# A hybrid diffusion backbone on one core: modulation sums on VectorE alone, five raw weight buffers, squares on ScalarE, and another order at the start of each block's second product

## The chip, the core and the metric

The kernel runs on one core of one Trainium2 chip. Its engines are TensorE (PE in the rows; its weight loads are PEld), VectorE (DVE), ScalarE (ACT), GpSimd (POOL), and SyncE (SP), which here only issues DMAs. The engines run side by side, each takes its own instructions strictly in the order of the program, and they wait for one another through semaphores. The metric is the time of the device in microseconds (us), the median over executions.

## What is computed

Two layers of a model over 512 latent tokens and 256 context tokens, of width 1024. Cut to what matters here:

```python
for layer in range(2):
    mod_x = silu(c) @ ada_w[layer] + ada_b[layer]        # 1024 x 6144 weights, for the latent tokens
    mod_c = silu(c_ctx) @ ada_w[layer] + ada_b[layer]    # the same weights, for the context tokens
    hx = rmsnorm(x, g1) * (1 + sc1) + sh1                # sh1, sc1, ... are sixths of mod_x
    x = x + gate1 * (mixer(hx) @ w_out[layer])           # retention and gated linear attention heads
    hx = rmsnorm(x, g2) * (1 + sc2) + sh2
    x = x + gate2 * (square(relu(hx @ w_mlp1[layer])) @ w_mlp2[layer])   # 1024 -> 4096 -> 1024
    # in layer 0 the context tokens go the same way, with mod_c
return rmsnorm(x)
```

All is float32. Products are made exact enough by splitting each operand into a rounded part (hi) and a remainder (lo), and adding three products: hi*hi, hi*lo, lo*hi. So each weight tile that lands raw has to be split: ScalarE makes hi by a cast, VectorE makes lo by a subtraction.

## The kernel before

Weights come in slabs of 128 x 1024 floats (512 KB). A slab is loaded by a DMA on SP's queue into one of NRAW = 4 raw buffers (pool `wraw`), and split into one of NSPL = 5 pairs of hi and lo buffers. `run` goes through a plan, a list of items in a fixed order; ahead of each item it splits slabs that later items need (`advance`), as far as a split buffer's last user has been issued, and loads slabs further ahead (`load_next`), as far as `limit = NRAW - (2 if ada_queue else 1) - order[loaded].raws` lets it: a slab counts as held from its load until its split is issued. The program order of every engine is the order in which this Python code issues.

The MLP of layer 0 is the stretch in question. Its 4096 hidden features are made in 8 blocks (u = 0 to 7) of 4 tiles of 128 features (m = 0 to 3). The first product of block u >= 1 is done by two pairs (`strassen_items`, a Strassen-Winograd scheme with seven products of half size): a pair takes two slabs of `w_mlp1` (`Pair`, two raw buffers at once, split in four parts) and makes two feature tiles for all 768 tokens. Its seven items in program order are p1, p6, p7, p5, p2, p4, p3. p1's bank of PSUM is copied to SBUF by ScalarE (line 1454) and p2 then adds to that bank; VectorE adds u2, u3, c22, c21 and c12 (line 1448), and p4 adds to the bank that u3 is read from. Each finished quarter goes through `hidden_chain`: relu on ScalarE (1425), the square rounded to hi on ScalarE (1426), the exact square on GpSimd (1427), lo = exact - hi on VectorE (1429). The second product of block u (`m2_part`) multiplies the 4 hidden tiles (its k tiles) by 4 slabs of `w_mlp2`; each slab holds two output tiles j. VectorE adds each result, times a gate, to the residual x (`residual`, line 641). Before, an item of the second product is one output tile in two banks (512 latent and 256 context tokens): in each bank first k = 0, 1, 2, then in each k = 3. Tiles k = 2 and 3 are those of the second pair, whose last quarter (c12) ends its chain last. In the last block an item is one output tile and one group of tokens.

Spread between these items is the modulation of layer 1 (`ada_sums`, called through `mlp_ada`): 64 tiles of `ada_w` (128 x 768, 384 KB, eight groups u of eight kk) are each loaded into a raw buffer and multiplied by a scalar per partition for each of the two conditions (v = 0, 1), and summed over kk; then nine small matmuls add over partitions. Before, v = 0 is summed by VectorE (405 for kk = 0, 407 after). For v = 1, ScalarE scales the tile (409 into a sum for kk < 2, else 411 in place, after VectorE has read it), and for kk >= 2 a DMA from GpSimd's queue adds the tile to one of two partial sums in SBUF (412). The load of the next tile is issued behind that. There are three calls of `mlp_ada` in each pair (after p6, p5 and p4) and eight in each second product of blocks 1 to 6. A group takes 11 calls: eight with a tile, two empty ones, and one with the small matmuls.

The other pools: `mp`, NSLOT = 47 slots of 768 floats per partition for activations, and PSUM with seven banks for products. `load_late` loads two constant tables, `delta` and `ramp`, once; `start` of each layer loads `cosT` and `sinT`.

Of the kernel before, what the change touches and what calls it, by code (L numbers as in the profile page):

```python
# [31 lines left out]
NSLOT = 47  # L32
NSPL = 5
NRAW = 4
# [103 lines left out]
def build(ctx: ExitStack, tc, a):  # L138
# [250 lines left out]
    def ada_sums(l):  # L389
        acc = [work(f"adaacc_{l}_{i}") for i in range(3)]  # L390
        todo = [(u, kk) for u in range(6 * D // T) for kk in range(KK)]

        def load(i):
            u, kk = todo[i]
            w = wraw.tile([P, WCOL], F32, tag="raw", name=f"adaw_{l}_{u}_{kk}")
            nc.sync.dma_start(w[:, 0:T], a["ada_w"][l, kk * P : (kk + 1) * P, u * T : (u + 1) * T])
            return w[:, 0:T]

        nxt = load(0)
        for i, (u, kk) in enumerate(todo):  # L400
            w = nxt
            c0, c1 = [cs[:, kk, v : v + 1] for v in range(2)]
            part = acc[1 + kk % 2]
            if kk == 0:
                nc.vector.tensor_scalar(acc[0], w, c0, None, op0=ALU.mult)
            else:
                nc.vector.scalar_tensor_tensor(acc[0], w, c0, acc[0], op0=ALU.mult, op1=ALU.add)  # L407
            if kk < 2:
                nc.scalar.mul(part, w, c1)
            else:  # L410
                nc.scalar.mul(w, w, c1)  # L411
                nc.gpsimd.dma_start(part, w, accum_op=ALU.add)  # L412
            if i + 1 < len(todo):
                nxt = load(i + 1)
            yield
            if kk == KK - 1:
                yield
                yield
                pt = psa.tile([P, 512], F32, tag="psa", name=f"ada_{l}_{u}")
                for j, v in enumerate((0, 1, 1)):  # L420
                    for c in range(3):
                        nc.tensor.matmul(
                            pt[32 * c : 32 * c + 32, 0:256], onehot[:, v], acc[j][:, 256 * c : 256 * c + 256],
                            start=(j == 0), stop=(j == 2),
                        )
                ada_state["end", l] = ch.start(ada_finish(l, pt, [6 * u + 2 * c for c in range(3)], 256))
                yield
# [278 lines left out]
    def load_late():  # L706
        for name, shape in (("delta", [P, P]), ("ramp", [P, 2, P])):
            late[name] = load_const(name, shape)
# [42 lines left out]
    def layer(l, norm):  # L751
# [11 lines left out]
        def start():  # L763
# [8 lines left out]
            tabs["ret"] = [pairs[h // 2][:, h % 2] for h in range(NH)]  # L772
            for name in ("cosT", "sinT"):
                late[name] = work(f"{name}_{l}")[:, 0:LAT]
                nc.sync.dma_start(late[name], a[name])
# [572 lines left out]
        def m2_part(u, jps, groups, last, batch=4):  # L1348


            def fn():
# [6 lines left out]
                for i in range(0, len(todo), batch):  # L1358
                    pts = [bank(f"pm2_{l}_{u}_{j}_{t0}") for j, s, c0, v, t0, t1 in todo[i : i + batch]]
                    for ks in (range(0, UT - 1), range(UT - 1, UT)):  # L1360
# [58 lines left out]
        def hidden_chain(c, a_, t0, relu):  # L1419
# [7 lines left out]
            nc.gpsimd.tensor_mul(c, c, c)  # L1427
# [74 lines left out]
        def m2_item(u, jps, groups=vwhole, last=False, ada=True, batch=4):  # L1502
# [3 lines left out]
                Item(f"m2.{u}.{jps}", m2_part(u, jps, groups, last, batch), [m2[u][x[0]] for x in jps])  # L1506
# [4 lines left out]
        if l == 0:  # L1511
# [20 lines left out]
            for u in range(1, NU):  # L1532
                for j in range(UT // 2 * u, UT // 2 * (u + 1)):
                    strassen_items(j)
                for q in tiles if u < NU - 1 else ():
                    m2_item(u, [q], batch=2)
            for g in range(2):
                for i, q in enumerate(tiles):
                    m2_item(NU - 1, [q], TG[g : g + 1], True)
                    if g == 1 and i == 1:  # L1540
# [167 lines left out]
```

## Time and profile before

| | before |
|---|---|
| median of 2 runs | 1837.45 us (1836.16 to 1838.75) |
| the profiled execution's own time | 1836.57 us |
| its span, first to last instruction | 1834.8 us |
| TensorE busy | 1653.0 us (90%), 9120 matmuls |
| VectorE busy | 1023.0 us (56%) |
| ScalarE busy | 735.2 us (40%) |
| GpSimd busy | 243.6 us (13%) |
| mean granted TensorE clock | 0.949 of 2.4 GHz |
| moved by DMA | 194.26 MB, mean 106 GB/s |

Times within the profile are counted from the start of the span. "Busy" is the time in which an engine has an instruction in work; matmuls overlap, so that a busy TensorE may still be below its peak. The idle time before an instruction is put down to the instruction or the DMA that ended it.

### The profile page before, as it was taken

The page shows a single profiled execution, that of the slowest core. Times are in us where ns is not written, and L with a number is a line of the kernel's source. Part 1 is how long each engine was busy: PE and PEld are TensorE (multiplying, and loading weights), DVE is VectorE, ACT ScalarE, POOL GpSimd, SP SyncE. Part 2 cuts the span into 40 slices and gives each one's busy share as a digit, 9 for nine tenths or more (in the row PEclk, how much of TensorE's full clock was granted, in tenths as well). Part 3 has the DMA queues.
Part 4 walks back from the last instruction along what each step waited for, and adds up shares of the span by engine and source line. Part 5 has one row for each costly group of instructions (what it writes and reads, how often), then busy time and mean ns, then how long its engine had stood idle before and what let it go on. Part 6 is the DMA issues. An engine that isn't in the chain of part 4 may idle for free. (4 is left out here: it accounts for less than half of the span.)

```text
span 1834.8 us, 23190 instructions
## 1 busy us (share of the span) xinstructions
PE 1653.0 (90%) x9120; PEld 1422.1 (78%) x9120; DVE 1023.0 (56%) x1656; ACT 735.2 (40%) x1231; POOL 243.6 (13%) x263
## 2 busy tenths in 40 slices
PE   6899999999997778797876788899999989999998
PEld 3678888888786767696866677778888988888887
DVE  6665754556864444565554554676856664334435
ACT  5526235635533332343423333646346442232322
POOL 2200111100201111111201111100121120010000
PEclk8999999999998979898888889999999999999999
DMA  9333431322135344365444352211213333322321
GB/s 333 105 128 137 136 106 63 108 72 71 56 91 128 97 113 121 109 179 132 128 114 104 101 150 103 92 52 58 69 47 104 104 108 99 103 92 92 104 81 46
DMA packets 67404, 194.26 MB, mean 106 GB/s; under 512 B 7296, under 2 KB 18880, under 8 KB 67296
## 3 DMA queue, kind: packets, MB, share of 16 engines
q1 hardware_dynamic: 58112, 166.42, 27.7%
q0 software_dynamic: 9184, 26.38, 7.0%
q8 instruction: 71, 1.16, 0.3%
q14 instruction: 37, 0.30, 0.0%
HBM read 169.70 MB, written 4.19 MB: 95 GB/s over the span
## 5 line engine op out<-in xcount | busy, mean ns | idle before, releaser
L532 PE MATMUL pm<-hidh,hi_m 128*128 128x512 f32 (+1 forms) x800 | 287.5, 359 | 40.0 <-ACT hidh L1426 40.0
L533 PE MATMUL pm<-hidl,hi_m 128*128 128x512 f32 (+1 forms) x800 | 286.6, 358 | 24.7 <-DVE hidl L1429 20.9
L534 PE MATMUL pm<-hidh,lo_m 128*128 128x512 f32 (+1 forms) x800 | 284.1, 355 | 0.0
L532 PEld LDWEIGHTS pm<-hidh,hi_m 128*128 128x128 f32 x800 | 157.1, 196 | 65.4 <-ACT hidh L1426 43.0
L533 PEld LDWEIGHTS pm<-hidl,hi_m 128*128 128x128 f32 x800 | 157.2, 196 | 48.0 <-DVE hidl L1429 24.0
L641 DVE SCALAR_TENSOR_TENSOR x<-pm,mod,x 128x512 f32<-128x512 f32 (+1 forms) x200 | 120.6, 641 | 131.0 <-PE pm L534 130.9
L534 PEld LDWEIGHTS pm<-hidh,lo_m 128*128 128x128 f32 x800 | 156.8, 196 | 19.9
L246 ACT CAST hi_m<-raw_m 128x1024 fp32r<-128x1024 f32 x100 | 104.0, 1040 | 106.5 <-PE pm L533 93.3
L411 ACT ACTIVATE adaw<-adaw,cs 128x768 f32<-128x768 f32 x48 | 44.9, 936 | 222.2 <-DVE adaacc L407 213.0
L247 DVE TENSOR_TENSOR lo_m<-raw_m,hi_m 128x1024 fp32r<-128x1024 f32 x98 | 120.1, 1226 | 23.1 <-ACT hi_m L246 19.9
L533 PE MATMUL pm<-yl,hi_m 128*128 128x512 f32 (+1 forms) x352 | 127.5, 362 | 2.1 <-DVE yl L627 2.1
L532 PE MATMUL pm<-yh,hi_m 128*128 128x512 f32 (+1 forms) x352 | 127.9, 363 | 0.0
L534 PE MATMUL pm<-yh,lo_m 128*128 128x512 f32 (+1 forms) x352 | 127.3, 362 | 0.5 <-DVE lo_m L247 0.5
L1327 DVE TENSOR_TENSOR hidl<-relu,hidh 128x512 fp32r<-128x512 f32 (+1 forms) x44 | 28.8, 658 | 159.8 <-POOL relu L1325 159.8
L1413 PE MATMUL pst<-yh,hi_m1s 128*128 128x384 f32 x224 | 82.2, 367 | 29.2 <-ACT p L1454 29.2
L407 DVE SCALAR_TENSOR_TENSOR adaacc<-adaw,cs,adaacc 128x768 f32<-128x768 f32 x56 | 58.1, 1038 | 76.4 <-DMA adaw<-in_ada_w 76.3
L412 POOL DMA_DIRECT2D adaacc<-adaw x48 | 42.3, 881 | 357.4 <-ACT adaw L411 253.7
L1325 POOL TENSOR_TENSOR relu<-relu 128x512 f32<-128x512 f32 (+1 forms) x44 | 42.3, 964 | 337.7 <-ACT hidh L1324 337.4
L1413 PE MATMUL pst<-yh,lo_m1s 128*128 128x384 f32 x224 | 80.5, 359 | 3.4 <-DVE lo_m1s L529 3.4
L1413 PE MATMUL pst<-yl,hi_m1s 128*128 128x384 f32 x224 | 80.2, 358 | 0.0
L247 DVE TENSOR_TENSOR lo_wi<-raw_wi,hi_wi 128x1024 fp32r<-128x1024 f32 x49 | 59.4, 1225 | 33.1 <-ACT hi_wi L246 33.1
L533 PEld LDWEIGHTS pm<-yl,hi_m 128*128 128x128 f32 x352 | 67.0, 190 | 12.9 <-DVE yl L627 2.9
(361 smaller groups left out, 4062.0 us busy)
## 6 DMA issues: line engine op xcount, KB each, us to landing
raw_m<-in_w_mlp SPq DMA_DIRECT2D x100, 512.0 KB, 3.5
raw_wi<-in_w_in SPq DMA_DIRECT2D x58, 512.0 KB, 3.5
adaw<-in_ada_w SPq DMA_DIRECT2D x64, 384.0 KB, 3.3
adaacc<-adaw POOLq DMA_DIRECT2D x48, 384.0 KB, 4.0
adaw<-in_ada_w SPq DMA_DIRECT2D x32, 512.0 KB, 4.6
raw_m1s<-in_w_mlp SPq DMA_DIRECT2D x28, 512.0 KB, 3.6
adaw<-in_ada_w SPq DMA_DIRECT2D x32, 256.0 KB, 6.2
raw_wo<-in_w_out SPq DMA_DIRECT2D x16, 512.0 KB, 3.4
```

What stands on the lines that cost most here:

```text
L246: nc.scalar.copy(self.hi, self.raw)
L247: self.engine.tensor_sub(self.lo, self.raw, f32(self.hi))
L407: nc.vector.scalar_tensor_tensor(acc[0], w, c0, acc[0], op0=ALU.mult, op1=ALU.add)
L411: nc.scalar.mul(w, w, c1)
L412: nc.gpsimd.dma_start(part, w, accum_op=ALU.add)
L532: nc.tensor.matmul(out, wh, xh, start=first, stop=False)
L533: nc.tensor.matmul(out, wh, xl, start=False, stop=False)
L534: nc.tensor.matmul(out, wl, xh, start=False, stop=last)
L641: nc.vector.scalar_tensor_tensor(xs[kk][:, t0:t1], pt[:, 0 : t1 - t0], mod[l][:, v, gate + kk : gate + kk + 1], xs[kk][:, t0:t1], op0=ALU. ...
L1325: nc.gpsimd.tensor_mul(r, r, r)
L1327: nc.vector.tensor_sub(a_.lo[:, t0:t1], r, f32(a_.hi[:, t0:t1]))
L1413: nc.tensor.matmul(pt[:, 0:H], wt[:, w], xt, start=first and k == 0 and i == 0, stop=k == KH - 1 and i == 2, skip_group_check=True,)
```

## The change

- `ada_sums`: both sums are made by VectorE, one instruction per tile and condition. The ScalarE multiplications and the DMAs from GpSimd's queue are gone, and so are the third sum buffer, the two empty calls of each group (nine calls a group instead of eleven) and three of a group's nine small matmuls.
- NRAW goes from 4 to 5. NSLOT goes from 47 to 46, and `delta` and `ramp` are no longer constants but are loaded by each layer's `start` into a slot.
- `hidden_chain`: the exact square moves from GpSimd to ScalarE, behind the rounded one.
- `m2_part` gets a `cut`: which k tiles come in the first round over the banks. Blocks 1 to 6 begin their second product with one item of two output tiles, four banks, k = 0 and 1 in all four and then k = 2 and 3, followed by two calls of `mlp_ada`; the other six items are as before. Block 7's items are two output tiles of one token group, also cut at 2.

```diff
--- before.py
+++ after.py
@@ -29,9 +29,9 @@
 GLA_SCALE = 64 ** -0.5
 UTS = (4, 4)
 WCOL = 1024
-NSLOT = 47
+NSLOT = 46
 NSPL = 5
-NRAW = 4
+NRAW = 5
 AHEAD = 4
 LOADS = 6
 
@@ -387,7 +387,7 @@
         nc.vector.memset(onehot[:, v, v : v + 1], 1.0)
 
     def ada_sums(l):
-        acc = [work(f"adaacc_{l}_{i}") for i in range(3)]
+        acc = [work(f"adaacc_{l}_{v}") for v in range(2)]
         todo = [(u, kk) for u in range(6 * D // T) for kk in range(KK)]
 
         def load(i):
@@ -399,29 +399,22 @@
         nxt = load(0)
         for i, (u, kk) in enumerate(todo):
             w = nxt
-            c0, c1 = [cs[:, kk, v : v + 1] for v in range(2)]
-            part = acc[1 + kk % 2]
-            if kk == 0:
-                nc.vector.tensor_scalar(acc[0], w, c0, None, op0=ALU.mult)
-            else:
-                nc.vector.scalar_tensor_tensor(acc[0], w, c0, acc[0], op0=ALU.mult, op1=ALU.add)
-            if kk < 2:
-                nc.scalar.mul(part, w, c1)
-            else:
-                nc.scalar.mul(w, w, c1)
-                nc.gpsimd.dma_start(part, w, accum_op=ALU.add)
+            for v in range(2):
+                c = cs[:, kk, v : v + 1]
+                if kk == 0:
+                    nc.vector.tensor_scalar(acc[v], w, c, None, op0=ALU.mult)
+                else:
+                    nc.vector.scalar_tensor_tensor(acc[v], w, c, acc[v], op0=ALU.mult, op1=ALU.add)
             if i + 1 < len(todo):
                 nxt = load(i + 1)
             yield
             if kk == KK - 1:
-                yield
-                yield
                 pt = psa.tile([P, 512], F32, tag="psa", name=f"ada_{l}_{u}")
-                for j, v in enumerate((0, 1, 1)):
+                for v in range(2):
                     for c in range(3):
                         nc.tensor.matmul(
-                            pt[32 * c : 32 * c + 32, 0:256], onehot[:, v], acc[j][:, 256 * c : 256 * c + 256],
-                            start=(j == 0), stop=(j == 2),
+                            pt[32 * c : 32 * c + 32, 0:256], onehot[:, v], acc[v][:, 256 * c : 256 * c + 256],
+                            start=(v == 0), stop=(v == 1),
                         )
                 ada_state["end", l] = ch.start(ada_finish(l, pt, [6 * u + 2 * c for c in range(3)], 256))
                 yield
@@ -704,8 +697,7 @@
     late = {}
 
     def load_late():
-        for name, shape in (("delta", [P, P]), ("ramp", [P, 2, P])):
-            late[name] = load_const(name, shape)
+        pass
 
 
     nrd = DEPTH * 2 * NH
@@ -770,6 +762,10 @@
 
             pairs = [work(f"rtab_{l}_{i}").rearrange("p (h w t) -> p h w t", h=2, w=3) for i in range(2)]
             tabs["ret"] = [pairs[h // 2][:, h % 2] for h in range(NH)]
+            t = work(f"pos_{l}")
+            late["delta"], late["ramp"] = t[:, 0:P], t[:, P : 3 * P].rearrange("p (d t) -> p d t", d=2)
+            for name in ("delta", "ramp"):
+                nc.sync.dma_start(late[name], a[name])
             for name in ("cosT", "sinT"):
                 late[name] = work(f"{name}_{l}")[:, 0:LAT]
                 nc.sync.dma_start(late[name], a[name])
@@ -1345,7 +1341,7 @@
 
             return fn
 
-        def m2_part(u, jps, groups, last, batch=4):
+        def m2_part(u, jps, groups, last, batch=4, cut=UT - 1):
 
 
             def fn():
@@ -1357,7 +1353,7 @@
                             todo.append((jp * (WCOL // P // UT) + jj, m2[u][jp], jj * UT * P, v, t0, t1))
                 for i in range(0, len(todo), batch):
                     pts = [bank(f"pm2_{l}_{u}_{j}_{t0}") for j, s, c0, v, t0, t1 in todo[i : i + batch]]
-                    for ks in (range(0, UT - 1), range(UT - 1, UT)):
+                    for ks in (range(0, cut), range(cut, UT)):
                         for pt, (j, s, c0, v, t0, t1) in zip(pts, todo[i : i + batch]):
                             project(pt, s, c0, hs, t0, t1, ks)
                     for pt, (j, s, c0, v, t0, t1) in zip(pts, todo[i : i + batch]):
@@ -1424,7 +1420,7 @@
             if relu:
                 nc.scalar.activation(c, c, AF.Relu)
             nc.scalar.activation(hh, c, AF.Square)
-            nc.gpsimd.tensor_mul(c, c, c)
+            nc.scalar.activation(c, c, AF.Square)
             yield
             nc.vector.tensor_sub(hl, c, f32(hh))
 
@@ -1499,11 +1495,11 @@
             if u and ada:
                 plan.append(Item("ada", mlp_ada))
 
-        def m2_item(u, jps, groups=vwhole, last=False, ada=True, batch=4):
+        def m2_item(u, jps, groups=vwhole, last=False, ada=True, batch=4, cut=UT - 1):
 
             jps = [(x, 0, WCOL // P // UT) if isinstance(x, int) else x for x in jps]
             plan.append(
-                Item(f"m2.{u}.{jps}", m2_part(u, jps, groups, last, batch), [m2[u][x[0]] for x in jps])
+                Item(f"m2.{u}.{jps}", m2_part(u, jps, groups, last, batch, cut), [m2[u][x[0]] for x in jps])
             )
             if not last and ada:
                 plan.append(Item("ada", mlp_ada))
@@ -1532,12 +1528,15 @@
             for u in range(1, NU):
                 for j in range(UT // 2 * u, UT // 2 * (u + 1)):
                     strassen_items(j)
-                for q in tiles if u < NU - 1 else ():
-                    m2_item(u, [q], batch=2)
+                if u < NU - 1:
+                    m2_item(u, [0], cut=2)
+                    plan.append(Item("ada", mlp_ada))
+                    for q in tiles[2:]:
+                        m2_item(u, [q], batch=2)
             for g in range(2):
-                for i, q in enumerate(tiles):
-                    m2_item(NU - 1, [q], TG[g : g + 1], True)
-                    if g == 1 and i == 1:
+                for i in range(UT):
+                    m2_item(NU - 1, [i], TG[g : g + 1], True, cut=2)
+                    if g == 1 and i == 0:
                         plan.append(Item("nx0", lambda: next_norm(nxt, l + 1, 0)))
             return plan, nxt
```

## Rows read from the trace of the kernel before

**Rows 1.** Page, part 1: busy time, share of the span and instructions of each engine.

```profile
PE 1653.0 (90%) x9120; PEld 1422.1 (78%) x9120; DVE 1023.0 (56%) x1656; ACT 735.2 (40%) x1231; POOL 243.6 (13%) x263
```

**Rows 2.** Windows: stretch, length, busy per engine (instructions), clock, DMA share, GB/s.

```profile
522.20:566.30 44.10, 32.52 (x176) 31.59 (x174) 27.59 (x38) 21.00 (x33) 9.78 (x11) 0.92 0.53 140
566.30:662.70 96.40, 74.94 (x381) 67.17 (x381) 46.66 (x69) 29.44 (x44) 13.98 (x16) 0.84 0.47 122
...
1026.40:1114.90 88.50, 72.81 (x400) 65.36 (x400) 44.74 (x70) 27.83 (x43) 12.18 (x14) 0.90 0.41 112
...
522.20:1114.90 592.70, 468.47 (x2496) 422.84 (x2494) 304.81 (x456) 195.73 (x291) 90.24 (x103) 0.88 0.46 122
```

**Rows 3.** Waits from 520 to 1120 us: who <- whom, total us, times, longest.

```profile
DVE adaacc L407 <- DMA adaw<-in_ada_w: 76.3, 28, 8.4
...
DVE lo_m1s L529 <- ACT hi_m1s L528: 47.5, 26, 2.7
...
PE pm L532 <- ACT hidh L1426: 40.0, 7, 8.8
...
PE pst L1413 <- DVE u L1448: 30.3, 8, 5.4
...
PE pst L1413 <- ACT p L1454: 29.2, 7, 6.9
...
PE pm L533 <- DVE hidl L1429: 20.9, 7, 3.5
...
DVE lo_m L247 <- ACT hi_m L246: 15.5, 8, 3.1
```

**Rows 4.** Timeline of one modulation tile: start, length, engine, line [idle before <-releaser].

```profile
627.31 1.02 DVE L407 SCALAR_TENSOR_TENSOR adaacc<-adaw,cs,adaacc 128x768 f32<-128x768 f32 x1 [7.58 <-DMA adaw<-in_ada_w]
...
637.17 1.02 DVE L407 SCALAR_TENSOR_TENSOR adaacc<-adaw,cs,adaacc 128x768 f32<-128x768 f32 x1 [3.58 <-DMA adaw<-in_ada_w]
...
628.36 0.94 ACT L411 ACTIVATE adaw<-adaw,cs 128x768 f32<-128x768 f32 x1 [7.51 <-DVE adaacc L407]
...
629.66 0.88 POOL L412 DMA_DIRECT2D adaacc<-adaw  x1 [7.90 <-PE pst L1413]
...
633.62 0.33 SPq L396 DMA_DIRECT2D adaw<-in_ada_w  x1
```

**Rows 5.** Line 396, the modulation tiles' loads: times from issue to landing.

```profile
DMA to landing us min/median/max: 3.1/3.3/4.7
```

**Rows 6.** Timeline where block 1's second product begins, TensorE, then VectorE, then ScalarE.

```profile
662.69 0.79 PE L532 MATMUL pm<-hidh,hi_m 128*128 128x512 f32 x1 [4.84 <-ACT hidh L1426]
666.68 0.80 PE L533 MATMUL pm<-hidl,hi_m 128*128 128x512 f32 x1 [3.20 <-DVE hidl L1429]
...
660.98 0.55 DVE L1448 TENSOR_TENSOR c<-pst,u 128x384 f32<-128x384 f32 x1
663.60 1.23 DVE L529 TENSOR_TENSOR lo_m1s<-raw_m1s,hi_m1s 128x1024 fp32r<-128x1024 f32 x1 [2.08 <-ACT hi_m1s L528]
...
666.07 0.55 DVE L1429 TENSOR_TENSOR hidl<-c,hidh 128x384 fp32r<-128x384 f32 x1
...
662.11 0.52 ACT L1426 ACTIVATE hidh<-c 128x384 fp32r<-128x384 f32 x1
```

**Rows 7.** Windows without a stall: seven items of a second product; two pairs (columns: rows 2).

```profile
767.50:796.60 29.10, 29.10 (x169) 25.59 (x168) 18.43 (x28) 7.33 (x10) 4.36 (x5) 1.00 0.60 134
796.70:827.80 31.10, 31.10 (x190) 29.79 (x189) 20.06 (x32) 14.94 (x24) 5.00 (x6) 1.00 0.54 167
```

**Rows 8.** The same two windows, line 407 alone: length, VectorE busy (instructions).

```profile
767.50:796.60 29.10, 7.09 (x7) 1.00 0.60 134
796.70:827.80 31.10, 2.28 (x2) 1.00 0.54 167
```

**Rows 9.** Groups by line from 520 to 1120 us: line, names, count | busy, mean ns.

```profile
L407 DVE SCALAR_TENSOR_TENSOR adaacc<-adaw,cs,adaacc 128x768 f32<-128x768 f32 x56 | 58.1, 1038 | 76.4 <-DMA adaw<-in_ada_w 76.3
...
L1427 POOL TENSOR_TENSOR c<-c 128x384 f32<-128x384 f32 x56 | 50.8, 908 | 182.5 <-ACT hidh L1426 167.0 <-issue 14.9
```

## Prediction

> **What bounds the kernel now.** I read the page's busy times first. TensorE is busy 90% of the span [rows 1], so only about a tenth of the time can be won from idle time, plus whatever a slow clock costs. Next come the windows, cut where the second products of layer 0's MLP begin. They show where that tenth lies: in the 592.7 us from 522.2 to 1114.9, TensorE is busy only 468.5 us and its granted clock is 0.88, that is, it sits at 1.2 GHz instead of 2.4 for part of the stretch [rows 2]. From one block's second product to the next takes (1114.9 - 566.3)/6 = 91.4 us; I call this a period.
>
> What would a period need? Seven items of a second product ran in 29.1 us without a stall, 4.16 us each, and two pairs in 31.1 us [rows 7]. A block with eight output tiles needs 8 x 4.16 + 31.1 = 64.4 us. So 27 us of each period are stalls and matmuls at the low clock.
>
> The waits of that stretch say what TensorE stands still for: the hidden tiles' hi (40.0 us, 7 times) and lo (20.9 us, 7 times), both once per block where its second product begins, and inside the pairs u3 from VectorE (30.3 us) and ScalarE's copy of p1 (29.2 us) [rows 3]. Together 120 us.
>
> Why are these late? VectorE itself stands 76.3 us for modulation tiles that have not landed [rows 3], and all that follows in its program waits with it. The timeline shows the loop of one tile: VectorE's sum at 627.31, ScalarE's multiplication at 628.36, GpSimd's issue of the accumulation at 629.66, and only at 633.62 SP's issue of the next load, which lets VectorE go on at 637.17 [rows 4]. That load waits for a buffer, and the buffer is free only when the accumulation has landed, 4 us after its issue. In the pairs two raw buffers hold the pair and one the next `w_mlp2` slab, so the modulation has a single one and a cycle of 637.17 - 627.31 = 9.9 us, against the 31.1/6 = 5.2 us that TensorE needs per call. The two windows without a stall are where the tiles fell kindly: in the pairs only two VectorE sums of line 407 fell [rows 8].
>
> **The sums.** Both conditions on VectorE cost two instructions of 1.02 us, 2.04 per tile [rows 4]. A load takes 3.3 us, at most 4.7 [rows 5]. The buffer is free as soon as VectorE has read it, so the cycle becomes 2.04 + 3.3 + 0.1 = 5.4 us instead of 9.9. ScalarE loses 64 multiplications of 0.94 us and GpSimd 48 issues of 0.88 [rows 4]; neither was the bound, but ScalarE no longer waits for VectorE there, so the wait for p1's copy should go. VectorE gains 64 x 1.04 = 66 us [rows 9]. A period holds 14 calls; eight of nine have a tile, so 12.4 tiles or 25 us of sums. Without its 9.1 us of line 407, VectorE was busy 46.7 - 9.1, about 37 us a period [rows 2, 9]; after, 62 of it against TensorE's 64.4. So VectorE becomes almost as loaded as TensorE.
>
> The Trainium skill speaks against this edit: Perfetto Trace Analysis, section Optimizing Scalar/DVE Operations, says that where VectorE is saturated, moving some of its work to ScalarE may make sense; the change does the reverse. The trace shows VectorE busy only half of a period before, and no run here shows yet whether 62 of 64 us counts as saturated; by that rule the third rival below gains.
>
> **The fifth buffer.** By the code's limit, a pair may now be loaded while another pair is held (5 - 1 - 2 = 2), and a slab while three are held. So the weights take four buffers nearly always, and the modulation still has one. I count the fifth at nothing in the sum: the 5.4 us cycle stays.
>
> The Trainium skill, Perfetto Trace Analysis, section Optimization Strategy, says that the same gap repeating on the engine that should be saturated can mean too few buffers for the next tile. The trace agrees so far that each block repeats the same gaps; if the added buffer ended them, the second rival would come true.
>
> **Squares.** An exact square takes 0.91 us on GpSimd [rows 9] and about 0.52 on ScalarE, as the rounded one does [rows 6]. That shortens a chain by 0.4 us, but ScalarE's next cast starts 0.5 us later. At the block boundary lo waits for that cast and for VectorE's splitting behind it: 662.69 (hi there), 663.60 (split), 666.07 (lo) [rows 6]. I count zero, from -0.4 to +0.5 us a block.
>
> **The cut.** Before, six matmuls of 512 columns stand between the last pair and the first need of its tiles, a third of an item: 1.4 us. After, half of a double item: 4.16 us. c12 at 660.98 to lo's end at 666.6 is 5.6 us [rows 6], with VectorE late besides.
>
> **Constants and slots.** Two more small loads in layer 1 stand before `cosT` on SP's queue, and a slot less: 0 to 3 us, taken as zero.
>
> **One period after.** (a) The first, double item: 8.3 us, some 5 us of waiting in it for c12's chain (5.6 us and about 3.5 by which VectorE is late, less 4.16), and 3 us at the low clock after it: 16.4. The 3 us come from the stretch: TensorE is busy 468.5 us where 31.1 + 6 x 64.4 = 417.5 would do [rows 2, 7], so the low clock takes 51 us, 7 a block, and a block has two to three stalls. (b) VectorE then goes through eight modulation calls, 7.1 with a tile: 7.1 x 5.4 + 0.9 x 1.6 (VectorE's other work per item, 11.34/7 [rows 7, 8]), less 3.4 since the first tile has long landed: 36 us. TensorE needs 8.3 + 7 items' worth less the first, 25 us, and the banks let it run that far ahead. So VectorE enters the pairs 11 us late, and p4 of the first pair, which needs u3, stands some 9 us. (c) In the pairs VectorE needs 20.06 - 2.28 - 0.6 = 17.2 us for its other work [rows 7, 8], 5.3 tiles' sums of 2.04 = 10.8, and some 5 us in which a load isn't covered by work: 33. (d) TensorE begins the next second product about 2 us before VectorE is through. 16.4 + 36 + 33 - 2 = 83 us, against 91.4.
>
> The calls end early: 72 are needed (eight groups of nine), against 88. Six come in block 1's pairs and 14 in each period, so five periods use them up. The fifth saves the pairs' sums: 79 us. The sixth has none: 64.4 and about 1 of stall, 65.5. Block 1's pairs take some 38 us instead of 44.1 [rows 2]; VectorE enters them without a lag.
>
> 38 + 4 x 83 + 79 + 65.5 = 514.5, against 592.7 [rows 2]: 78 us less. Outside this stretch I change nothing. The profiled execution took 1836.57 us, the median is 1837.45, 0.9 more; 1836.6 - 78 = **1758 us**.
>
> **Rivals.** *TensorE keeps its pace.* If the modulation gets a second buffer often enough, or VectorE's loads and work overlap well, a period is 64.4 and some 4 us at the boundary, 68.5; the first stretch 33.5. 33.5 + 6 x 68.5 = 444.5, 148 less: 1688 us. For it: seven VectorE sums in a second product cost TensorE nothing [rows 7, 8]. Against: the limit of the code, and 62 us of work for VectorE.
>
> *VectorE also waits for ScalarE's halves.* VectorE stood 47.5 and 15.5 us for ScalarE's casts before its subtractions [rows 3], 10 us a period. I left this out of (b) and (c), as a late VectorE finds its casts made. If it doesn't, a period is 93, and 38 + 4 x 93 + 89 + 65.5 = 564.5: 28 us less, 1808 us, no difference worth the name.
>
> *Slower.* Four held weight slabs mean that a modulation tile's load is issued behind them more often. Each us by which a landing is later costs about 11 us a period (7.1 loads in (b), four in (c)). To lose 37 us in all, a period must reach 106, so a landing 2.1 us later: 5.4 us on average. The longest of 64 was 4.7 [rows 5], the median 3.3, so this needs a new mean above the old longest. At a mean of 5.6 a period is 108 and the time about 1883 us.
>
> **Chances.** Forecast 0.54, pace kept 0.24, casts 0.18, slower 0.04. A difference under 2% (37 us) is about what a measurement can't tell from none. The forecast (its own range 1723 to 1793, a period 7 us shorter or longer) and the pace kept are faster: 0.78. The casts are the same: 0.18. Slower: 0.04. The range goes from 1668, the pace kept with almost no stall (periods of 65), to 1812, just past the casts; it leaves out slower, a third of the casts and the tails of the rest, about 0.19.
>
> **What would show it.** Right: in the stretch VectorE's wait for modulation tiles stays, in pieces of 1 to 3 us; SP's issue of such a load follows VectorE's second sum at once; p1's copy is no longer waited for; u3 is, once per block, in the first pair; the last period is near 65 us. Wrong: if a period with tiles lasts under 72 us, the modulation had more than one buffer or VectorE enough room; if over 90, VectorE's waits for ScalarE or for landings are the cause, which the waits tell apart. A change outside 522 to 1115 us would show that slots or the constants' loads matter.

## The result, and the profile of the changed kernel

| | before | after |
|---|---|---|
| median of 2 runs | 1837.45 us | 1777.59 us (1776.35 to 1778.82) |
| span of the profiled execution | 1834.8 us | 1777.0 us |
| from the start of block 1's pairs to the last block's second product | 592.7 us [rows 2] | 539.0 us |

The ratio is 0.9674, 95% interval 0.9633 to 0.9716: 3.3% faster, 60 us, where 78 were forecast. In the changed kernel the lines quoted here from L415 on stand 4 to 7 lower: the three products are L525 (hi, waits for `hidh`), L526 (waits for `hidl`) and L527, the small modulation matmuls L415, `hidh` L1422, the exact square L1423, `hidl` L1425, u and c L1444, p1's copy L1450, the residuals L634.

The page first: busy time of each engine, and then all that DMAs moved.

```profile
PE 1634.8 (92%) x9072; PEld 1404.2 (79%) x9072; DVE 1076.0 (61%) x1720; ACT 707.8 (40%) x1223; POOL 152.8 (9%) x159
...
DMA packets 60777, 175.56 MB, mean 99 GB/s; under 512 B 6560, under 2 KB 18400, under 8 KB 60672
```

Against [rows 1] VectorE has 53 us more work (66 were forecast), GpSimd 91 us less, and 48 matmuls are gone: the third sum no longer has to be added by TensorE (three matmuls a group in the code, two instructions each in the trace). 18.7 MB less are moved, about the 48 accumulations of 384 KB. The windows (columns as in [rows 2]) show where the time was won: in the MLP of layer 0, as forecast. The first row is the whole stretch, the next two are block 2's second product and block 3's pairs, the fourth is the last period, and the last two are what lies outside.

```profile
519.10:1058.10 539.00, 453.49 (x2455) 407.11 (x2453) 355.93 (x520) 167.63 (x282) 0.00 (x0) 0.93 0.33 99
...
640.70:690.10 49.40, 39.30 (x208) 32.40 (x207) 31.08 (x46) 9.04 (x14) 0.00 (x0) 0.90 0.32 96
690.10:725.80 35.70, 31.32 (x171) 30.68 (x170) 27.01 (x38) 15.54 (x27) 0.00 (x0) 0.95 0.39 118
...
986.10:1058.10 72.00, 63.18 (x349) 58.23 (x349) 37.20 (x56) 24.52 (x41) 0.00 (x0) 0.95 0.18 59
...
0.00:519.10 519.10, 486.96 (x2913) 402.05 (x2914) 319.11 (x572) 247.87 (x460) 66.10 (x68) 0.98 0.36 119
1058.10:1777.00 718.90, 694.38 (x3708) 595.03 (x3708) 400.92 (x629) 292.33 (x482) 86.70 (x91) 0.98 0.26 84
```

The stretch is 53.7 us shorter: 38.7 of them are idle time of TensorE (592.7 - 468.5 = 124.2 before, 539.0 - 453.5 = 85.5 after), and 15.0 busy time, by a granted clock of 0.93 instead of 0.88 and the 48 matmuls. Ahead of the stretch 3.1 us were won (522.2 to 519.1), behind it 1.0 (719.9 to 718.9). The waits of the stretch (who <- whom, total us, times, longest):

```profile
DVE adaacc L407 <- DMA adaw<-in_ada_w: 50.3, 29, 3.3
...
DVE lo_m1s L522 <- ACT hi_m1s L521: 33.1, 17, 2.6
PE pm L526 <- DVE hidl L1425: 25.8, 7, 4.1
PE pm L525 <- ACT hidh L1422: 22.8, 7, 4.7
PE ada L415 <- DVE adaacc L407: 19.5, 12, 6.0
PE pst L1409 <- DVE u L1444: 9.4, 6, 2.9
...
PE pst L1409 <- ACT p L1450: 5.0, 3, 2.3
PE adat L333 <- ACT adarow L328: 5.0, 4, 2.7
DVE lo_m L247 <- ACT hi_m L246: 4.0, 13, 0.4
```

Beside [rows 3], the pairs' waits (u and p1's copy) went from 59.5 to 14.4 us and `hidh` from 40.0 to 22.8. `hidl` did not get less (20.9 to 25.8). And a wait stands there that the kernel before hardly had: TensorE waits 19.5 us in front of the small matmuls for VectorE's sums, and 5.0 for the transposes that follow them (L333). One second product shows how that comes about: SyncE's issues, then VectorE's sums, then TensorE.

```profile
630.21 1.93 SPq L288 DMA_DIRECT2D raw_m1s<-in_w_mlp  x2
...
642.91 2.34 SPq L288 DMA_DIRECT2D raw_m1s<-in_w_mlp  x2
659.86 21.42 SPq L396 DMA_DIRECT2D adaw<-in_ada_w  x6
...
656.78 1.20 DVE L634 SCALAR_TENSOR_TENSOR x<-pm,mod,x 128x512 f32<-128x512 f32 x2 [1.41 <-PE pm L527]
657.90 1.94 DVE L407 SCALAR_TENSOR_TENSOR adaacc<-adaw,cs,adaacc 128x768 f32<-128x768 f32 x2
663.01 1.95 DVE L407 SCALAR_TENSOR_TENSOR adaacc<-adaw,cs,adaacc 128x768 f32<-128x768 f32 x2 [3.18 <-DMA adaw<-in_ada_w]
...
673.67 1.95 DVE L407 SCALAR_TENSOR_TENSOR adaacc<-adaw,cs,adaacc 128x768 f32<-128x768 f32 x2 [2.22 <-DMA adaw<-in_ada_w]
...
678.98 1.95 DVE L407 SCALAR_TENSOR_TENSOR adaacc<-adaw,cs,adaacc 128x768 f32<-128x768 f32 x2 [1.17 <-DMA adaw<-in_ada_w]
...
682.97 2.00 PE L415 MATMUL ada<-adaacc,onehot 128*32 128x256 f32 x12 [4.60 <-DVE adaacc L407]
```

This is block 2's second product. The slabs of block 3's first pair are loaded at 630.21, and those of its second pair already at 642.91, while the first pair still holds its two buffers. Then the weights have four buffers and the modulation one: the next tile's load is issued at 659.86, as the second sum ends (657.90 + 1.94), and a tile takes 663.01 - 657.90 = 5.1 us. That is the 5.4 us of the forecast. What the forecast missed is the last row: TensorE meets the small matmuls in its program and stands 4.60 us for the sums.

The other stall, where that second product begins (TensorE, then ScalarE, then VectorE):

```profile
646.52 0.50 PE L525 MATMUL pm<-hidh,hi_m 128*128 128x512 f32 x1 [1.46 <-ACT hidh L1422]
651.07 0.79 PE L526 MATMUL pm<-hidl,hi_m 128*128 128x512 f32 x1 [4.04 <-DVE hidl L1425]
...
646.50 0.52 ACT L1423 ACTIVATE c<-c 128x384 f32<-128x384 f32 x1
646.93 1.03 ACT L521 CAST hi_m1s<-raw_m1s 128x1024 fp32r<-128x1024 f32 x1
...
647.99 1.23 DVE L522 TENSOR_TENSOR lo_m1s<-raw_m1s,hi_m1s 128x1024 fp32r<-128x1024 f32 x1 [2.63 <-ACT hi_m1s L521]
649.13 0.69 DVE L297 TENSOR_TENSOR s_m1s<-raw_m1s,raw_m1s 128x512 f32<-128x512 f32 x1
649.86 0.69 DVE L298 TENSOR_TENSOR raw_m1s<-raw_m1s 128x512 f32<-128x512 f32 x1
650.46 0.55 DVE L1425 TENSOR_TENSOR hidl<-c,hidh 128x384 fp32r<-128x384 f32 x1
```

The exact square is there at 647.02, but VectorE makes `hidl` only at 650.46: the splitting of the next pair's slab stands in front of it in program order, and that waits for a cast which ScalarE does behind the square. No modulation tile takes part. In [rows 6] the order was the same (the split at 663.60, `hidl` at 666.07), with VectorE late besides.

### The profile page after: what moved, and what is told of

It is laid out like the page before. It is cut to its first block, busy times and chain, and to the rows that moved or that the text cites. A ratio compares the mean times of both kernels' runs of the same rounds, so it can differ in the third digit from the quotient of the medians.

```text
span 1777.0 us, 22807 instructions
## 1 busy us (share of the span) xinstructions
PE 1634.8 (92%) x9072; PEld 1404.2 (79%) x9072; DVE 1076.0 (61%) x1720; ACT 707.8 (40%) x1223; POOL 152.8 (9%) x159
## 3 DMA queue, kind: packets, MB, share of 16 engines
q1 hardware_dynamic: 58400, 166.62, 29.2%
## 4 chain that ended last, share of the span: by engine, by line
PE 64%; DVE 17%; ACT 8%; DMA 6%; issue 5%; SPq 0%; POOL 0%; DVEq 0%; ACTq 0%; POOLq 0%
PE pm L526 10%; PE pm L527 10%; PE pm L525 10%; DMA adaw<-in_ada_w 5%; DVE adaacc L407 4%; PE ps_g L527 2%; PE ps_g L525 2%; PE ps_g L526 2%; PE pro L1128 1%; DVE x L634 1%; PE ps_vr L526 1%; PE ps_vr L525 1%; PE ps_vr L527 1%; DVE lo_m L247 1%; PE ps_vg L525 1%
## 5 line engine op out<-in xcount | busy, mean ns | idle before, releaser
L526 PE MATMUL pm<-hidl,hi_m 128*128 128x512 f32 (+1 forms) x800 | 288.5, 361 | 29.6 <-DVE hidl L1425 25.8
L525 PE MATMUL pm<-hidh,hi_m 128*128 128x512 f32 (+1 forms) x800 | 288.5, 361 | 22.8 <-ACT hidh L1422 22.8
L527 PE MATMUL pm<-hidh,lo_m 128*128 128x512 f32 (+1 forms) x800 | 285.9, 357 | 0.0
L526 PEld LDWEIGHTS pm<-hidl,hi_m 128*128 128x128 f32 x800 | 157.6, 197 | 53.3 <-DVE hidl L1425 28.3
L525 PEld LDWEIGHTS pm<-hidh,hi_m 128*128 128x128 f32 x800 | 157.5, 197 | 48.5 <-ACT hidh L1422 24.4
L634 DVE SCALAR_TENSOR_TENSOR x<-pm,mod,x 128x512 f32<-128x512 f32 (+1 forms) x200 | 121.3, 641 | 112.3 <-PE pm L527 112.3
L527 PEld LDWEIGHTS pm<-hidh,lo_m 128*128 128x128 f32 x800 | 157.2, 197 | 20.5
L407 DVE SCALAR_TENSOR_TENSOR adaacc<-adaw,cs,adaacc 128x768 f32<-128x768 f32 x112 | 108.8, 1013 | 50.3 <-DMA adaw<-in_ada_w 50.3
L526 PE MATMUL pm<-yl,hi_m 128*128 128x512 f32 (+1 forms) x352 | 128.0, 364 | 2.1 <-DVE yl L620 2.1
L525 PE MATMUL pm<-yh,hi_m 128*128 128x512 f32 (+1 forms) x352 | 128.3, 365 | 0.0
L527 PE MATMUL pm<-yh,lo_m 128*128 128x512 f32 (+1 forms) x352 | 127.7, 363 | 0.5 <-DVE lo_m L247 0.5
L1409 PE MATMUL pst<-yh,hi_m1s 128*128 128x384 f32 x224 | 76.9, 343 | 5.0 <-ACT p L1450 5.0
L526 PEld LDWEIGHTS pm<-yl,hi_m 128*128 128x128 f32 x352 | 67.4, 192 | 13.0 <-DVE yl L620 2.9
L247 DVE TENSOR_TENSOR lo_wi<-raw_wi,hi_wi 128x1024 fp32r<-128x1024 f32 x49 | 59.2, 1224 | 29.1 <-ACT hi_wi L246 29.1
L1409 PE MATMUL pst<-yl,hi_m1s 128*128 128x384 f32 x224 | 76.2, 340 | 0.0
L527 PEld LDWEIGHTS pm<-yh,lo_m 128*128 128x128 f32 x352 | 67.4, 191 | 10.9 <-DVE lo_m L247 1.0
L1409 PE MATMUL pst<-yh,lo_m1s 128*128 128x384 f32 x224 | 75.9, 339 | 0.0
L525 PEld LDWEIGHTS pm<-yh,hi_m 128*128 128x128 f32 x352 | 67.4, 191 | 10.1
L1319 ACT ACTIVATE relu<-pm 128x512 f32<-128x512 f32 (+1 forms) x44 | 23.6, 537 | 128.8 <-PE pm L527 128.8
```

The costliest lines, as they stand in the source:

```text
L247: self.engine.tensor_sub(self.lo, self.raw, f32(self.hi))
L407: nc.vector.scalar_tensor_tensor(acc[v], w, c, acc[v], op0=ALU.mult, op1=ALU.add)
L525: nc.tensor.matmul(out, wh, xh, start=first, stop=False)
L526: nc.tensor.matmul(out, wh, xl, start=False, stop=False)
L527: nc.tensor.matmul(out, wl, xh, start=False, stop=last)
L634: nc.vector.scalar_tensor_tensor(xs[kk][:, t0:t1], pt[:, 0 : t1 - t0], mod[l][:, v, gate + kk : gate + kk + 1], xs[kk][:, t0:t1], op0=ALU. ...
```

## The experiments

All ratios are to the kernel before, run on the same chip; its medians there were 1837.9 to 1838.4 us.

| kernel | median us | ratio, 95% interval |
|---|---|---|
| before + new sums alone | 1774.02 | 0.9646 (0.9626 to 0.9666) |
| before + new order alone | 1821.89 | 0.9896 (0.9872 to 0.992) |
| changed, four raw buffers | 1756.18 | 0.9553 (0.9529 to 0.9577) |
| changed, old order | 1780.89 | 0.9685 (0.9668 to 0.9703) |
| changed, exact squares on GpSimd | 1778.38 | 0.966 (0.9634 to 0.9687) |
| changed, two empty calls back | 1763.46 | 0.9591 (0.9573 to 0.9609) |
| changed, four buffers, empty calls back | 1760.55 | 0.9565 (0.9543 to 0.9587) |
| changed, two buffers kept for the modulation | 1741.36 | 0.9463 (0.9442 to 0.9485) |
| the same, old order | 1757.27 | 0.956 (0.9546 to 0.9574) |
| the same, half of the sums | 1730.53 | 0.9411 (0.9397 to 0.9425) |
| the same, `hidl` ahead of the next split | 1716.47 | 0.934 (0.9324 to 0.9355) |
| changed, `hidl` ahead of the next split | 1756.52 | 0.9564 (0.9547 to 0.9581) |

### The sums, alone

Into the kernel before, only the new `ada_sums` (two VectorE instructions a tile, no empty calls).

> The kernel before, with the modulation sums alone changed (both on VectorE, nine calls a group). Theory: the tile cycle falls from 9.9 to 5.4 us, the waits for u3 and for p1's copy fall as in the kernel after, the boundaries keep their 61 us, and the new wait for the last sums comes in: about 1837 - 30 = 1807 us. Rival: without the other parts VectorE's 66 us more work cost as much as the shorter cycle brings: 1830 us or more.

64 us faster, so neither had it: that is as much as the whole change (60 us) or a little more. VectorE's wait for tiles in the stretch fell from 76.3 us [rows 3] to 20.8, in pieces of at most 2.2:

```profile
DVE adaacc L407 <- DMA adaw<-in_ada_w: 20.8, 17, 2.2
```

That is less than half of the 50.3 us of the changed kernel. So the tiles come faster with four buffers than with five, and the single buffer that the forecast gave the modulation after the change is not what the sums alone have.

### Four raw buffers

```diff
-NRAW = 5
+NRAW = 4
```

> The kernel after, with four raw buffers instead of five. Theory: the fifth buffer goes to the weights, and the modulation has one buffer in the pairs either way, so it is worth nothing: 1772 to 1783 us, cycle of a modulation tile 5.1 to 5.4 us as after. Rival: the fifth buffer carries a good part of the gain of 60 us: 1795 us or more.

Both were wrong: the fifth buffer, counted at nothing in the forecast, costs 21.4 us. SyncE's issues in the same second product say why; here it runs from 639.7 to 682.5:

```profile
635.28 4.65 SPq L288 DMA_DIRECT2D raw_m1s<-in_w_mlp  x2
641.93 28.31 SPq L396 DMA_DIRECT2D adaw<-in_ada_w  x7
672.83 3.24 SPq L288 DMA_DIRECT2D raw_m1s<-in_w_mlp  x2
```

With four buffers the limit doesn't let the second of the next two pairs in until late (672.83 instead of 642.91), so that in the second product a second buffer is free, and seven tiles are loaded one behind the other with VectorE never waiting for one. The wait in front of the small matmuls is 7.0 us there instead of 19.5 (over all blocks). With five, the weights take the added buffer and the one that was free besides. The whole stretch takes 514.2 us instead of 539.0 (columns as above):

```profile
523.70:1037.90 514.20, 446.45 (x2454) 403.63 (x2452) 356.21 (x520) 168.11 (x281) 0.00 (x0) 0.94 0.34 104
```

The price of the fifth buffer hangs on the order, too. With the old order, the changed kernel with five buffers took 1780.89 us, and the sums alone with four 1774.02; apart from the squares and the slots these two differ in the buffer, so there it costs some 7 us.

### The empty calls

```diff
             if kk == KK - 1:
+                yield
+                yield
                 pt = psa.tile([P, 512], F32, tag="psa", name=f"ada_{l}_{u}")
```

> The kernel after, with the two empty modulation calls put back between a group's last sum and its small matmuls (11 calls a group, as before). Theory: TensorE comes to the small matmuls before VectorE has made the last sum and waits 19.5 us there, 5 more at the transposes behind them, and runs at the low clock afterwards; two calls later the sums are done. So this should take about 1777 - 25 = 1752 us, with no wait of line 415 for line 407. Rival: VectorE is simply behind, and the same lateness shows at the next wait (u3, or the hidden tiles): 1770 us or more.

14.1 us, between the two theories. With the calls back (two lines more, so L1411 is L1409 and L1446 L1444) the small matmuls come two items later, and TensorE no longer waits for L407 there. The wait does not go altogether: u and the transposes behind the small matmuls (L333) are waited for longer.

```profile
PE pst L1411 <- DVE u L1446: 11.3, 8, 2.9
PE adat L333 <- ACT adarow L328: 10.3, 4, 3.9
```

19.5 + 9.4 + 5.0 = 33.9 us became 21.6, so 12.3 of the 14.1. With four buffers the same calls should be worth nothing if the tiles' cycle is the cause:

> The kernel after with four raw buffers and with the two empty modulation calls back. Theory: the two are separate waits, the small matmuls' 7.0 us that are left with four buffers and the transposes' 3.4 go with some low clock: 1756 - 12 = 1744 us. Rival: with four buffers VectorE is late no more where the small matmuls come, and the calls are worth nothing: 1753 us or more.

They bring nothing there, as the rival had it: 1760.55 against 1756.18 us, with ranges that overlap (1757.5 to 1762.7, 1754.8 to 1759.5), and the profiled stretch took 514.7 against 514.2. TensorE's wait went from the small matmuls (7.0 to 0 us) to u (10.4 to 18.5). So the empty calls pay only where the second products leave the modulation a single buffer.

### Two buffers kept for the modulation

```diff
-            limit = NRAW - (2 if ada_queue else 1) - order[loaded].raws
+            limit = NRAW - 2 - order[loaded].raws
```

> The kernel after, still with five raw buffers, but the weights may hold three at most (one line, the limit of the loads), so that the modulation always has two. Theory: the fifth buffer cost 21 us because it let the weights take the modulation's second buffer in the second products (a cycle of 5.2 us on one buffer against 4.2 us an output tile); with two kept free this takes no longer than with four buffers, 1756 us or less, and VectorE's wait for tiles that have not landed falls from 50 us below 15. Rival: what costs is the deeper queue of weight loads or the fifth buffer's place, not the modulation's share: 1770 us or more.

36.2 us less than the changed kernel and 14.8 less than with four buffers: a fifth buffer helps once it goes to the tiles. No wait of VectorE for a tile is left in the stretch. Block 2's second product takes 42.5 us instead of 49.4 (columns as above), and in it a timeline row shows two tiles summed with no pause:

```profile
629.20:671.70 42.50, 36.95 (x207) 31.39 (x206) 30.93 (x46) 9.15 (x14) 0.00 (x0) 0.92 0.37 112
```
```profile
645.83 3.79 DVE L407 SCALAR_TENSOR_TENSOR adaacc<-adaw,cs,adaacc 128x768 f32<-128x768 f32 x4
```

The Trainium skill, Perfetto Trace Analysis, section Optimization Strategy, says that the same gap repeated on the engine that should be saturated can mean that there are not enough buffers. The runs agree only in part: one more buffer cost 21.4 us, and the same buffer handed to the loads that were late brought 14.8.

### The order, three times

The order of before put back into the changed kernel:

```diff
-                if u < NU - 1:
-                    m2_item(u, [0], cut=2)
-                    plan.append(Item("ada", mlp_ada))
-                    for q in tiles[2:]:
-                        m2_item(u, [q], batch=2)
+                for q in tiles if u < NU - 1 else ():
+                    m2_item(u, [q], batch=2)
```

> The kernel after, with the second products in the order of before (one output tile an item, k = 0, 1, 2 first). Theory: each of 7 boundaries loses 4.16 - 1.4 = 2.8 us of cover, and with the low clock some 4 us: about 1777 + 25 = 1802 us; TensorE's waits for the hidden tiles go from 48.6 to some 68 us. Rival: VectorE is late by more than either cover, so that the order is worth nothing: under 1785 us.

3.3 us, in the range of the rival. The wait for `hidh` does rise as the edit says, from 22.8 to 41.9, but that in front of the small matmuls falls from 19.5 to 8.0:

```profile
PE pm L525 <- ACT hidh L1422: 41.9, 7, 8.1
...
PE ada L415 <- DVE adaacc L407: 8.0, 9, 2.6
```

The new order alone, in the kernel before:

> The kernel before, with the second products' new order alone. Theory: undoing it in the kernel after cost only 3 us, as VectorE is later than either cover, and before the change it is later still: 1830 to 1838 us, with TensorE's waits for the hidden tiles still over 45 us. Rival: in the kernel before the boundary waits (61 us) are the larger part, and 2.8 us more cover at each of seven pays in full: 1815 us or less.

16 us, between the two: the wait for `hidh` falls from 40.0 us [rows 3] to 20.9. And undone where two buffers are kept:

> The kernel with two buffers kept for the modulation (1741.4 us), with the order before put back: the second product begins with three quarters of its first tile's products instead of half of two tiles'. Theory: the cut gives TensorE 2.8 us more of work between the last pair and the need of its tiles (4.16 less 1.4), and VectorE is no longer late here, so that each of 7 boundaries loses that much when it is undone: 1755 to 1763 us. Rival: what the cut covers comes back as the wait for hidl behind it, as it did with five buffers and one kept, where undoing it cost 3 us: 1740 to 1748 us.

15.9 us. So the order is worth 16 us, most of the 7 x 2.8 us of cover in the forecast, both in the kernel before and where tiles are never late. Only in the changed kernel, where the second products too leave the tiles a single buffer, does it come to 3.

### Squares back on GpSimd

```diff
-            nc.scalar.activation(c, c, AF.Square)
+            nc.gpsimd.tensor_mul(c, c, c)
```

> The kernel after, with the exact square of the pairs back on GpSimd. Theory: worth nothing, 1777 us within 5 either way; at the boundary lo waits for the splitting ahead of it in VectorE's program, not for the square. Rival: GpSimd's 0.9 us and its sharing with VectorE carry some of the gain: 1785 us or more.

0.8 us, no difference. Zero was right, and both of the forecast's effects show: with the squares on GpSimd TensorE waits less for `hidl` (20.8 us instead of 25.8) and more for `hidh` (27.2 instead of 22.8).

### Half of the sums

```diff
-                else:
+                elif v == 0:
```

> The kernel with two buffers kept for the modulation (1741.4 us), leaving out the second condition's sum for all tiles but the first of each group of eight, so one VectorE instruction of 1.02 us per tile less: the second condition's modulation is wrong by that. Theory: with two buffers VectorE has room for the sums, and taking 56 of 128 away (57 us of VectorE's time) gives the end at most 10 us: 1731 to 1742 us. Rival: VectorE, at 377 us of the 538 in this stretch, is in fact what the pairs wait for (u, hidh, hidl), and its lag shrinks with each sum taken away: 1725 us or less.

10.8 us, just past the edge of the theory: 56.5 us of VectorE's work are worth a fifth of themselves. The wait for u went from 8.0 to 2.6 us.

### `hidl` ahead of the next pair's split

```diff
+                plan.append(Item("tick", lambda: None))
                 if u < NU - 1:
                     m2_item(u, [0], cut=2)
```

The plan gets an empty item, so that the chain of the last quarter goes one step on before the next item's slabs are split.

> The kernel with two buffers kept for the modulation (1741.4 us), and in each block one empty item put between its last pair and its second product, so that VectorE gets the subtraction hidl of the block's last quarter ahead of the next pair's splitting of m1s. Theory: there TensorE stands about 4 us in each of 7 blocks (25.6 us in all) for hidl, and of the 4.0 us shown in one boundary 3.4 is VectorE's wait for ScalarE's cast (L521) and three instructions on m1s (L522, L297, L298) that stand in front of hidl by program order alone. With hidl first the wait falls to 1 us or less each and the time to 1712 to 1725. Rival: hidl is late because its squares on ScalarE are late, or the next pair's splitting, now later, is missed further on; then the time is 1735 or more.

24.9 us. The square at 633.12 is followed at once by `hidl`, and the split comes behind it. The last two rows are the wait for `hidl` without the empty item and with it:

```profile
633.12 0.52 ACT L1423 ACTIVATE c<-c 128x384 f32<-128x384 f32 x1
...
633.68 0.56 DVE L1425 TENSOR_TENSOR hidl<-c,hidh 128x384 fp32r<-128x384 f32 x1 [1.70 <-ACT c L1423]
634.61 1.23 DVE L522 TENSOR_TENSOR lo_m1s<-raw_m1s,hi_m1s 128x1024 fp32r<-128x1024 f32 x1 [0.38 <-ACT hi_m1s L521]
```
```profile
PE pm L526 <- DVE hidl L1425: 25.6, 7, 4.0
...
PE pm L526 <- DVE hidl L1425: 4.0, 7, 0.7
```

The wait fell from 25.6 to 4.0 us, and nothing later misses the split. This is the fastest kernel here: 6.6% under the kernel before.

I had put the lost worth of the order down to the tile cycle: what TensorE wins where the block begins, it would wait in front of the small matmuls. The same empty item in the changed kernel itself tests that.

> The changed kernel (1777.6 us: five buffers, one kept for the modulation) with the empty item in front of each block's second product, so that hidl goes ahead of the next pair's splitting. With two buffers kept the same edit gave 24.9 us. Theory: here a tile each 5.1 to 5.4 us sets the length of the second product, and TensorE, which begins it 3.4 us earlier, only waits that much longer for VectorE in front of the small matmuls: the wait for hidl falls from 25.8 us to some 4, the wait of the small matmuls rises above 19.5 by 10 us or more, and the time is 1765 to 1778 us. Rival: the two waits have nothing to do with each other, and the gain is that with two buffers: 1750 to 1757 us.

The rival was right: 21.1 us, nearly as with two buffers, and the wait in front of the small matmuls stayed.

```profile
PE ada L415 <- DVE adaacc L407: 19.4, 12, 6.0
...
PE pm L526 <- DVE hidl L1425: 3.1, 7, 0.7
```

So the theory of a fixed length was wrong. VectorE's first tile of a second product comes behind the residuals of its first item (L634, then L407 in the rows above), and so the row of tiles starts earlier when TensorE does. In the kernel with the item it starts at 650.41, 13.2 us after the second product's beginning at 637.2; in the changed kernel 17.2 us after it (657.90, 640.7). With the old order it is 656.89 - 641.5 = 15.4 us, though `hidh` is waited for 2.8 us longer there (4.29 instead of 1.46): the single first item ends sooner than the double one. That agrees with the order being eaten up by the tiles behind it. No run changed the length of the first item by itself, so this reading of the 3 us remains argued.

## Why the prediction was right and where it was not

The direction, the place and the time within its own range (1723 to 1793) held; 1758 was 20 us too low. That it came so near is in part luck: terms that were wrong in opposite directions cancel, as shown below.

| from `hidh` to `hidh` | forecast us | measured us |
|---|---|---|
| block 1's pairs | 38 | 42.7 |
| four periods | 83 each | 84.7, 87.5, 84.1, 90.5 |
| fifth | 79 | 77.6 |
| last | 65.5 | 71.9 |
| sum | 514.5 | 539.0 |

- **The sums: right.** The cycle is 5.1 to 5.4 us, the load is issued as the second sum ends, p1's copy is waited for 5.0 us instead of 29.2, and VectorE is busy 31.08 + 27.01 = 58 us in the period from 640.7, against 62 forecast. Alone they bring 64 us. The Trainium skill, Perfetto Trace Analysis, section Optimizing Scalar/DVE Operations, says that moving work off VectorE may make sense where it is saturated; the changed kernel's VectorE is busy 66% of the stretch (355.93 of 539.0), and in the kernel with two buffers kept, leaving out 56.5 us of its sums brought 10.8 us, so nothing here shows it saturated.
- **The fifth buffer: the failed step.** "I count the fifth at nothing" compared one buffer with one buffer. One was right for five raw buffers, but with four the second products have two, since the second of the next two pairs can't be loaded so early. The sentence was read off the pairs [rows 4], where it holds, and carried over to the second products, where it doesn't. [rows 8] had it already: seven tiles in 29.1 us of a second product, where a single buffer gave one in 9.9 [rows 4]. It measured 21.4 us.
- **Where the lag is paid: wrong.** Step (b) let TensorE run ahead through the second product and put 9 us a block on p4 in the first pair, some 45 in all. u took 9.4 us in six waits, and with p1's copy 14.4. TensorE is held earlier, at the small matmuls: 19.5 + 5.0 us. The forecast had seen that the two empty calls go, but not that the small matmuls then stand directly behind the last sum in TensorE's program. The longest period, 90.5, beyond the bound of 90 that the forecast gave itself, has the longest such wait, 6.0 us, and 13.6 us of VectorE waiting for tiles.
- **The boundary: mis-sized.** Step (a) had some 5 us of waiting per block and took 3.5 of it for VectorE's lag, so that the last period, without tiles, was to have 1 us. It is (25.8 + 22.8) / 7 = 6.9 us, and the last period has 72.0 - 63.18 = 8.8. For `hidl`, 3.4 of the 4.0 us in the boundary shown is program order; the empty item took away 3.1 a block (25.6 to 4.0 us in seven).
- **Cover, squares.** The cover's size (2.8 us a block) was about right where the order could pay it out (2.3); squares at zero were right. Constants and slots were to cost 0 to 3 us; outside the stretch 4.1 us were gained instead. The part of it ahead of the stretch goes with the fifth buffer: in the profiles of the nine kernels with five, block 1's pairs begin at 519.0 to 521.8 us, in those of the five with four at 522.2 to 526.7, whether the slots are the old ones or the new.
- **The rivals.** VectorE's waits for casts did not all vanish (47.5 to 33.1 and 15.5 to 4.0 us), but they matter at one place, the split ahead of `hidl`. Landings were no later (3.1 to 4.6 us), so the slower case had no ground. "TensorE keeps its pace" named a second buffer as its condition; with it, and `hidl` ahead, block 2's second product and block 3's pairs take 39.1 + 34.0 = 73.1 us, where 68.5 was worked out:

```profile
627.30:666.40 39.10, 36.94 (x208) 31.38 (x207) 30.97 (x46) 9.15 (x14) 0.00 (x0) 0.96 0.40 122
666.40:700.40 34.00, 31.10 (x171) 30.64 (x170) 28.66 (x40) 15.54 (x27) 0.00 (x0) 0.95 0.43 135
```

The sum fell 24.5 us short. By its own terms, that is some 11 us net of waiting (24.5 at the small matmuls and 18 at the boundaries more, 31 in the pairs less); the other 13 I put down to the low clock behind these stalls, by subtraction only. The busy time points the same way: TensorE is busy 453.5 us, 36 above the forecast's 417.5 at full clock, where step (a) had 3 us a block for it. With four buffers the stretch takes 514.2 us, where 514.5 was forecast, and that is luck: TensorE's waits at the boundaries are 43 us there and those for u and p1's copy 16, where some 31 and 45 were forecast.

From kernel to kernel: 1838.1 - 64.1 (sums) - 17.8 (order, squares and slots, with four buffers, from 1774.0 to 1756.2) + 21.4 (fifth buffer) = 1777.6. That sum holds by the way it is made, and the parts hang on one another: the fifth buffer costs some 14 us more with the new order than with the old, which is the worth that the order loses with five buffers.

## What to carry to other kernels

Count buffers stage by stage: one that is added goes to whoever asks first, and a prefetch that asks early can take the one that the slower stream lived on, so look at which loads the queue issues, and when. When a delay is taken out between an engine's result and the in-order engine that consumes it, look at what that engine will now meet in its program before the result is there. A stall that stays the same in every block, also in one without the suspected work, may be program order: look at what stands in front of the late instruction on its own engine.

## What the chip showed that was not expected

A stall of 4 us on TensorE costs more than its 4 us. Behind the one at 651.07 the granted clock was 0.50 for the whole of the next 3.3 us, the 1.2 GHz level, and matmuls of 512 columns took 0.63 us:

```profile
651.07:654.40 3.33, 3.33 (x10) 2.85 (x11) 0.75 (x1) 0.00 (x0) 0.00 (x0) 0.50 0.02 5
```
```profile
651.66 0.63 PE L527 MATMUL pm<-hidh,lo_m 128*128 128x512 f32 x1
```

From 655.89 on they took 0.39 again, and the granted clock was 1.00. At that clock the 4.8 us in between would have been about half as long, so the wait cost some 2.4 us more (an estimate from the two levels). Taking 21.6 us of such waits away brought 24.9 us. But shorter stalls did not keep the clock up: with `hidl` ahead, after waits of 1.51 and 0.66 us, it was still down, 0.56 from 634 to 637.

```profile
634.00:637.00 3.00, 2.71 (x8) 2.23 (x9) 2.59 (x4) 0.58 (x1) 0.00 (x0) 0.56 0.04 15
```
